# State space tables started after the first u columns; x rows, x^T buffers, row factors and the sine rearranged

## The chip, the cores and the metric

The kernel runs on one NeuronCore of a Trainium2 chip. The metric is the device time of one launch in microseconds. One core has five engines with a queue of instructions each: TensorE (PE; its weight loads are listed as PEld), VectorE (DVE), ScalarE (ACT), GpSimd (POOL) and SyncE (SP), which here issues nearly all DMAs. Each engine takes its own instructions in their order; an instruction that waits holds up everything behind it on that engine.

## The reference, cut to what matters

One layer of a decoder trunk on x of 2048 tokens by 1024 columns, all in float32:

```
h    = RMSNorm(x); P = h @ W_in              # columns for three groups of heads
o_A  = sliding window attention (window 128) of P's columns a
o_B  = S5 state space mixer of P's columns u (512 of them, 32 groups of 16 channels, 64 complex states each)
o_C  = compressed + selected + window attention of P's columns b and c
x    = x + concat(norm(o_A), norm(o_B), norm(o_C)) @ W_out
x    = x + relu(RMSNorm(x) @ W_up)^2 @ W_down
```

The mixer needs tables that depend on its parameters alone, not on x: dt = exp(log_dt), the powers of A_bar = exp(A dt) (magnitude by an exponential, angle by sine and cosine of 11 doublings of the angle), B_bar = (A_bar - 1)/A * B, and products of C with those powers.

## The kernel before, in words

The order of the instructions is set by a scheduler that follows the order in which the Python code emits steps, lists of steps that `merge` interleaves evenly, and priorities; `tc.high_priority` lets an instruction go earlier. A tile pool with n buffers makes the n+1st tile wait for the release of the first. A pool opened where a closed one lay waits for the users of that memory. DMAs that SP issues also wait, in SP's order, for what their target buffer or their completion counter needs.

`phase_front` (line 81) computes P in two halves of 8 row groups (128 tokens with stride 16 each). For one row group, `load_h` (line 103) loads the transposed block of x (`xT`, 512 KB, from a copy of x transposed beforehand) and splits it into a rounded part `hh` (ACT, line 109) and a rest `hl` (DVE, line 110). `load_w` does the same for a column chunk of W_in, one of 8 row blocks k at a time: `raw` by DMA, `wh` (ACT, line 146), `wl` (DVE, line 147). `product` (line 151) multiplies a row group with a chunk: 24 matmuls, three for each k, into one of two PSUM buffers, which ACT then empties. The chunks of a half come in the order u (256 columns), u (256), a (384), b (384), c (396).

The normalising factor of each token is applied to the product. Its sum of squares comes from the rows of x themselves (`row_sum`, line 113, a load and an ACT square per row group), the reciprocal root of 8 row groups from `row_factors` (line 118, 14 small instructions on GpSimd). In the first half the u columns are stored unscaled, and `scaled` (line 122) multiplies them afterwards.

`ssm_tables` (line 282) is a generator with 12 stops. Before, its first eight parts are merged with the first chunk's steps of the first half, and the other four with the second chunk's. `exp_acc` (line 229) is the exponential on DVE (once on 32 columns, names e1..., once on 544, names e2...), `sincos` (line 254) reduces the angle on DVE and calls the sine on ACT twice, for sine and for cosine. `pair_steps` (line 431) then makes, for 16 pairs of groups, the product tables oCA (three DVE instructions of 128x544 each, lines 442 to 444), two matmuls pk with the table k_Y (line 451) and their stores; it is merged with the chunks a, b and c. `extra` makes six bias vectors, one matmul each, after the second chunk.

In the second half, `ssm_steps` (line 467) uses the tables. All later phases (attention, output product, the two products of the feed forward) follow.

Of the kernel before, what the change touches and what calls it, by code (L numbers as in the profile page):

```python
# [7 lines left out]
F32 = mybir.dt.float32  # L8
F32R = mybir.dt.float32r
I32 = mybir.dt.int32  # L10
AF = mybir.ActivationFunctionType
ALU = mybir.AluOpType
# [4 lines left out]
P = 128  # L17
D = 1024
# [17 lines left out]
G = 32  # L36
WIDTHS = {"a": 390, "b": 388, "c": 398}
TWO_PI = 2.0 * math.pi
# [18 lines left out]
def rsqrt_into(nc, pool, y, ss, scale, n, tag, eng=None):  # L57
    h = pool.tile([P, n], F32, tag=tag + "h", name=tag + "h")
    t = pool.tile([P, n], F32, tag=tag + "t", name=tag + "t")
    rsqrt_steps(eng or nc.vector, y, ss, h, t, scale)  # L60


def run(steps):
    for st in steps:
        st()


def merge(*lists):

    order = sorted(((k + 0.5) / len(l), n, k) for n, l in enumerate(lists) for k in range(len(l)))  # L70
    return [lists[n][k] for _, n, k in order]
# [9 lines left out]
def phase_front(tc, C, x, norm1_g, w_in, u_st, pd, rh_a, prm, dkp, dca, consts, extra, x_t):  # L81

    nc = tc.nc
    with ExitStack() as ctx:
        kp = ctx.enter_context(tc.tile_pool(name="skp", bufs=1))
# [31 lines left out]

        def row_factors(half):
            sl = slice(8 * half, 8 * half + 8)
            rsqrt_into(nc, rp, rx[:, sl], ss[:, sl], 1.0 / D, 8, "rq", nc.gpsimd)  # L120

        def scaled(s):
            u = u_st[:, :, u_cols(s)]
# [58 lines left out]
        S = {}  # L182
        for half in range(2):
            box, hs = {}, []

            def steps_of(ch):
                kind, c0, n = ch
                res = [lambda: box.update({ch: load_w(half, *ch)})]
                if ch is chunks[0]:
                    res.insert(0, lambda: hs.append(load_h(8 * half)))  # L190
                for j in range(8):
                    if ch is chunks[0] and j < 7:
                        res.append(lambda j=j: hs.append(load_h(8 * half + j + 1)))
                    for part in ((0, 1) if half and kind != "u" else (None,)):
                        res.append(lambda j=j, part=part: product(8 * half + j, hs[j], box[ch], kind, c0, n, part))
                return res
            lists = [steps_of(ch) for ch in chunks]
            with tc.tile_pool(name=f"a_x{half}", bufs=2, **({} if half else {"reuse_waits": "tile"})) as xp:
                box_x[:] = [xp]
                if half:  # L200
                    run(lists[0] + lists[1] + lists[2][:1])
                else:
                    gen = ssm_tables(tc, C, S, kp, prm, dkp)
                    run(lists[0][:3] + [consts] + merge(lists[0][3:], [lambda: next(gen)] * TABLE_PARTS[0]))
                if half:
                    nc.vector.tensor_copy(xp.tile([1, 1], F32, name="gate", bufs=1), box[chunks[2]][3][1][0:1, 0:1].bitcast(F32))
            if half == 0:
                c_rp = ctx.enter_context(ExitStack())
                rp = c_rp.enter_context(tc.tile_pool(name="a_r", bufs=2, reuse_waits="tile"))
                sums = [[lambda s=s: row_sum(s) for s in range(8 * n, 8 * n + 8)] + [lambda n=n: row_factors(n)] for n in range(2)]  # L210
                scales = [lambda s=s: scaled(s) for s in range(8)]
                run(merge(lists[1], sums[0], [lambda: next(gen, None)] * TABLE_PARTS[1]))
                with tc.tile_pool(name="bv", bufs=1, reuse_waits="tile") as bv:
                    extra(bv, ps_t)
                c_pre = ctx.enter_context(ExitStack())
                pre = c_pre.enter_context(tc.tile_pool(name="pre", bufs=1, side="right", reuse_waits="tile"))
                pairs = pair_steps(tc, C, S, dkp, dca, pre, ps_g)
                run(merge(merge(lists[2], scales) + merge(lists[3], sums[1]) + lists[4], pairs))
                c_rp.close()
            else:  # L220
                c_pre.close()
                tp = ctx.enter_context(tc.tile_pool(name="sg", bufs=2))
                lists[3].insert(8, lambda: head_norms(nc, rh_a, *hn_tiles(sp, "hn"), (pd["a"], 384, 6)))
                rest = sum(lists[2:], [])[1:]
                run(merge(rest, ssm_steps(tc, C, S, u_st, dkp, dca, tp, ps_g, ps_t)))
                store(0)
# [24 lines left out]
    return k  # L251


def sincos(nc, pool, s, c, x, shape, tag):

    def tl(n):
        return pool.tile(shape, F32, tag=tag + n, name=tag + n)
    k, r = tl("k"), tl("r")
    magic = 12582912.0
    nc.vector.tensor_scalar(k, x, 1.0 / TWO_PI, magic, op0=ALU.mult, op1=ALU.add)  # L260
    nc.vector.tensor_scalar(k, k, magic, None, op0=ALU.subtract)
    c1 = 6.28125
    c2 = float(int((TWO_PI - c1) * 2.0 ** 20)) / 2.0 ** 20
    c3 = TWO_PI - c1 - c2
    nc.vector.scalar_tensor_tensor(r, k, -c1, x, op0=ALU.mult, op1=ALU.add)
    nc.vector.scalar_tensor_tensor(r, k, -c2, r, op0=ALU.mult, op1=ALU.add)
    nc.vector.scalar_tensor_tensor(r, k, -c3, r, op0=ALU.mult, op1=ALU.add)
    pi = 3.1415925
    nc.vector.tensor_scalar(r, r, pi, -pi, op0=ALU.min, op1=ALU.max)
    nc.scalar.activation(s, r, AF.Sin)  # L270
    nc.vector.tensor_scalar(r, r, math.pi / 2.0, None, op0=ALU.add)
    nc.vector.tensor_scalar(k, r, pi, -TWO_PI, op0=ALU.is_gt, op1=ALU.mult)
    nc.vector.tensor_tensor(r, r, k, op=ALU.add)
    nc.vector.tensor_scalar(r, r, pi, -pi, op0=ALU.min, op1=ALU.max)
    nc.scalar.activation(c, r, AF.Sin)


TABLE_PARTS = (8, 4)
# [3 lines left out]
def ssm_tables(tc, C, S, pool, prm, dkp):  # L282
# [17 lines left out]
    def tmp(shape, n):  # L300
        return tp.tile(shape, F32, tag="t_" + n, name="t_" + n)

    with ExitStack() as ctx:
        tp = ctx.enter_context(tc.tile_pool(name="si", bufs=1))
        sn, cs = tmp([P, 11, G], "sn"), tmp([P, 11, G], "cs")

        ar, ai, ldt = tmp([P, G], "ar"), tmp([P, G], "ai"), tmp([P, G], "ldt")
        nc.sync.dma_start(ldt, log_dt[0:1].to_broadcast([P, G]))
# [17 lines left out]
        th = tmp([P, 11, G], "th")  # L326
        for j in range(11):
            nc.vector.tensor_scalar(th[:, j], adi, float(2 ** j), None, op0=ALU.mult)
        sincos(nc, tp, sn, cs, th, [P, 11, G], "sc")

        yield
        pr, pi_ = (tp.tile([P, 17, G], F32, tag="e2" + n, name="t_p" + n) for n in ("xc", "r"))
# [98 lines left out]
def pair_steps(tc, C, S, dkp, dca, tp, ps):  # L431
# [5 lines left out]
    def outer(b):  # L437
        bc = [P, GB, 17, 16]
        CA = M["c", b] = tp.tile(bc, F32, tag="oCA", name=f"oCA{b}", bufs=4)
        t1 = tp.tile(bc, F32, tag="ot", name=f"ot{b}", bufs=2)  # L440
        ar, ai = (S[n][:, :, group_slice(b)].rearrange("p t g -> p g t").unsqueeze(3).broadcast_to(bc) for n in ("AR", "AI"))
        nc.vector.tensor_tensor(CA, ar, S["C1"][:, group_slice(b)].unsqueeze(2).broadcast_to(bc), op=ALU.mult)
        nc.vector.tensor_tensor(t1, ai, S["C2"][:, group_slice(b)].unsqueeze(2).broadcast_to(bc), op=ALU.mult)
        nc.vector.tensor_tensor(CA, CA, t1, op=ALU.add)
# [1421 lines left out]
```

## Time and profile before

| | |
|---|---|
| median of 3 runs | 2589.37 us (2584.4 to 2590.45) |
| profiled execution, its own time | 2586.87 us |
| its span, first to last instruction | 2585.0 us |
| busy: PE, PEld | 2468.3 us (95%), 2073.2 us (80%) |
| busy: DVE, ACT, POOL | 1787.2 us (69%), 1334.9 us (52%), 1044.5 us (40%) |
| mean granted TensorE clock | 0.982 |

The span is divided into 40 slices of 64.6 us in the page. TensorE is at 9 tenths or more in nearly all of them; the first slice, 6 tenths, and the second, 8, are the start of `phase_front`. DVE is at 8 and 6 tenths there.

How to read it: busy shares are averages over stages. A wait is put down to what came last by the profile. Matmuls are pipelined and their ends are modelled, so the start of the next one tells more than the duration. An engine's idle time matters only where another waits for what stands behind it.

### The profile page before, as it was taken

The page shows a single profiled execution, that of the slowest core. Times are in us where ns is not written, and L with a number is a line of the kernel's source. Part 1 is how long each engine was busy: PE and PEld are TensorE (multiplying, and loading weights), DVE is VectorE, ACT ScalarE, POOL GpSimd, SP SyncE. Part 2 cuts the span into 40 slices and gives each one's busy share as a digit, 9 for nine tenths or more (in the row PEclk, how much of TensorE's full clock was granted, in tenths as well). Part 3 has the DMA queues.
Part 4 walks back from the last instruction along what each step waited for, and adds up shares of the span by engine and source line. Part 5 has one row for each costly group of instructions (what it writes and reads, how often), then busy time and mean ns, then how long its engine had stood idle before and what let it go on. Part 6 is the DMA issues. An engine that isn't in the chain of part 4 may idle for free. (4 is left out here: it accounts for less than half of the span.)

```text
span 2585.0 us, 38037 instructions
## 1 busy us (share of the span) xinstructions
PE 2468.3 (95%) x12766; PEld 2073.2 (80%) x12766; DVE 1787.2 (69%) x3466; ACT 1334.9 (52%) x2767; POOL 1044.5 (40%) x1047
## 2 busy tenths in 40 slices
PE   6899999999899999999989999899999999999999
PEld 6799997777787777778868888688887888888887
DVE  8643876864776677787566565755557887898886
ACT  4453555754666656565455554544444443344442
POOL 0100222221333333233366667565655354454447
PEclk8999999999899999999999999999999999999999
DMA  6463435321312112121356667755447534444335
GB/s 186 139 205 94 111 95 155 97 69 46 119 40 70 66 46 86 51 66 56 121 191 195 199 184 207 221 166 153 145 131 248 167 102 131 135 131 127 122 102 196
DMA packets 391075, 334.06 MB, mean 129 GB/s; under 512 B 42166, under 2 KB 355132, under 8 KB 389056
## 3 DMA queue, kind: packets, MB, share of 16 engines
q1 hardware_dynamic: 353696, 305.42, 38.9%
q10 hardware_dynamic: 37184, 26.22, 3.1%
q8 instruction: 101, 1.65, 0.3%
q14 instruction: 94, 0.77, 0.1%
HBM read 219.10 MB, written 112.45 MB: 128 GB/s over the span
## 5 line engine op out<-in xcount | busy, mean ns | idle before, releaser
L1341 ACT CAST v<-vr 128x512 fp32r<-128x512 f32 x224 | 139.3, 624 | 303.1 <-DMA vr<-vd 139.6
L1342 DVE TENSOR_TENSOR v<-vr,v 128x512 fp32r<-128x512 f32 x224 | 233.3, 1049 | 78.9 <-ACT v L1341 76.5
L1656 PE MATMUL pdc<-dw,v 128*128 128x512 f32 x768 | 186.3, 392 | 5.4 <-ACT dw L1341 4.1
L1656 PE MATMUL pda<-dw,v 128*128 128x512 f32 x768 | 184.5, 389 | 0.0
L1656 PE MATMUL pdb<-dw,v 128*128 128x512 f32 x768 | 184.5, 389 | 0.0
L1656 PEld LDWEIGHTS pdc<-dw,v 128*128 128x128 f32 x768 | 144.9, 189 | 36.8 <-ACT dw L1341 4.5
L1656 PEld LDWEIGHTS pdb<-dw,v 128*128 128x128 f32 x768 | 144.1, 188 | 30.0
L1656 PEld LDWEIGHTS pda<-dw,v 128*128 128x128 f32 x768 | 144.1, 188 | 30.0
L1452 POOL TENSOR_TENSOR fs<-ur,ur 128x512 f32<-128x512 f32 x64 | 96.8, 1512 | 163.9 <-DMA ur<-in_w_up 117.4
L1341 ACT CAST uh<-fs 128x512 fp32r<-128x512 f32 x128 | 78.6, 621 | 150.1 <-PE pub L1481 64.0
L1342 DVE TENSOR_TENSOR ul<-fs,uh 128x512 fp32r<-128x512 f32 x128 | 134.9, 1057 | 19.6 <-ACT uh L1341 19.5
L1342 DVE TENSOR_TENSOR ul<-ur,uh 128x512 fp32r<-128x512 f32 x96 | 98.8, 1032 | 50.3 <-ACT uh L1341 43.6
L76 PE MATMUL pw<-wo_h,mh 128*128 128x512 f32 x256 | 110.4, 431 | 4.7 <-DVE ml L1211 2.5
L546 POOL TENSOR_TENSOR t<-Q,E 128x508 f32<-128x508 f32 x16 | 21.4, 1341 | 230.9 <-ACT Q L526 200.2
L864 DVE TENSOR_TENSOR tls<-pps,ths 128x512 fp32r<-128x512 f32 (+1 forms) x144 | 92.8, 658 | 29.9 <-ACT ths L863 22.2
L1497 POOL TENSOR_TENSOR ev<-e,e 128x512 f32<-128x512 f32 x64 | 94.9, 1483 | 38.3 <-ACT e L1494 28.1
L863 ACT CAST ths<-pps 128x512 fp32r<-128x512 f32 (+1 forms) x144 | 79.2, 565 | 57.4 <-PE pps L860 26.6
L1481 PE MATMUL pub<-fl,uh 128*128 128x512 f32 x256 | 102.5, 401 | 3.3 <-DVE fl L1342 3.3
L77 PE MATMUL pw<-wo_l,mh 128*128 128x512 f32 x256 | 105.0, 410 | 0.0
L78 PE MATMUL pw<-wo_h,ml 128*128 128x512 f32 x256 | 104.7, 410 | 0.0
L1481 PE MATMUL pub<-fh,uh 128*128 128x512 f32 x256 | 102.8, 401 | 1.2 <-ACT fh L1341 1.2
L1481 PE MATMUL pua<-fh,uh 128*128 128x512 f32 x256 | 101.3, 396 | 2.3 <-ACT e L1501 2.3
(562 smaller groups left out, 7886.2 us busy)
## 6 DMA issues: line engine op xcount, KB each, us to landing
vr<-vd SPq DMA_DIRECT2D x224, 256.0 KB
ur<-in_w_up SPq DMA_DIRECT2D x128, 256.0 KB
vd<-ev SPq DMA_DIRECT2D x128, 256.0 KB
vd<-e ACTq DMA_DIRECT2D x64, 256.0 KB
dr<-in_w_down SPq DMA_DIRECT2D x32, 512.0 KB
x<-in_x SPq DMA_DIRECT2D x16, 512.0 KB
mx<-in_x SPq DMA_DIRECT2D x16, 512.0 KB
x<-mx ACTq DMA_DIRECT2D x16, 512.0 KB
```

Of the source, the lines that this page charges most:

```text
L76: nc.tensor.matmul(out, sh, mh, start=first, stop=False)
L77: nc.tensor.matmul(out, sh, ml, start=False, stop=False)
L78: nc.tensor.matmul(out, sl, mh, start=False, stop=last)
L546: nc.gpsimd.tensor_tensor(t[:, :, :, 0:n], Q[:, :, :, 0:n], e.rearrange("p g j c -> p j g c")[:, :, :, 0:n], op=ALU.mult)
L863: nc.scalar.copy(th[:, 0:nb], pt[:, 0:nb])
L864: nc.vector.tensor_tensor(tl[:, 0:nb], pt[:, 0:nb], th[:, 0:nb], op=ALU.subtract)
L1341: nc.scalar.copy(dh, src)
L1342: nc.vector.tensor_tensor(dl, src, dh, op=ALU.subtract)
L1452: nc.gpsimd.tensor_tensor(t, x, y, op=op)
L1481: nc.tensor.matmul(bank[b], w[:, k], h[o][:, k], start=first and k == 0 and n == 0, stop=k == HALF - 1 and n == 2, skip_group_check=True)
L1497: nc.gpsimd.tensor_tensor(tile_("v" + o), x, y, op=op)
L1656: nc.tensor.matmul(bank[b, q], x[:, q, j], y[:, j], start=first and j == 0 and n == 0, stop=j == 1 and n == 2, skip_group_check=True)
```

## The change

The tables now begin behind the whole first chunk, merged with the second chunk (eight parts) and with the first half of the chunk a (four parts); the pairs are merged with what is left of a, and with b and c. The pool of the x rows moves to the other side of SBUF, so it no longer lies where the x^T pool was, and its loads are merged from the second chunk on as before. The x^T pool has three buffers in the first half. The row factors are made by VectorE, with high priority. Sine and cosine are one ACT instruction on 704 columns. The buffer `ot` of the pairs is single, and their pool closes before the second half begins.

```diff
         def row_factors(half):
             sl = slice(8 * half, 8 * half + 8)
-            rsqrt_into(nc, rp, rx[:, sl], ss[:, sl], 1.0 / D, 8, "rq", nc.gpsimd)
+            with tc.high_priority(offset=W_HOIST):
+                rsqrt_into(nc, rp, rx[:, sl], ss[:, sl], 1.0 / D, 8, "rq")
...
-            with tc.tile_pool(name=f"a_x{half}", bufs=2, **({} if half else {"reuse_waits": "tile"})) as xp:
+            with tc.tile_pool(name=f"a_x{half}", bufs=2 if half else 3, **({} if half else {"reuse_waits": "tile"})) as xp:
                 box_x[:] = [xp]
                 if half:
                     run(lists[0] + lists[1] + lists[2][:1])
                 else:
-                    gen = ssm_tables(tc, C, S, kp, prm, dkp)
-                    run(lists[0][:3] + [consts] + merge(lists[0][3:], [lambda: next(gen)] * TABLE_PARTS[0]))
+                    run(lists[0])
...
             if half == 0:
-                c_rp = ctx.enter_context(ExitStack())
-                rp = c_rp.enter_context(tc.tile_pool(name="a_r", bufs=2, reuse_waits="tile"))
+                c_rp, c_pre = (ctx.enter_context(ExitStack()) for _ in range(2))
+                rp = c_rp.enter_context(tc.tile_pool(name="a_r", bufs=2, side="right", reuse_waits="tile"))
                 sums = [[lambda s=s: row_sum(s) for s in range(8 * n, 8 * n + 8)] + [lambda n=n: row_factors(n)] for n in range(2)]
                 scales = [lambda s=s: scaled(s) for s in range(8)]
-                run(merge(lists[1], sums[0], [lambda: next(gen, None)] * TABLE_PARTS[1]))
+                gen = ssm_tables(tc, C, S, kp, prm, dkp)
+                consts()
+                run(merge(lists[1], sums[0], [lambda: next(gen)] * TABLE_PARTS[0]))
+                l2 = merge(lists[2], scales)
+                n2 = len(l2) // 2
+                run(merge(l2[:n2], [lambda: next(gen, None)] * TABLE_PARTS[1]))
                 with tc.tile_pool(name="bv", bufs=1, reuse_waits="tile") as bv:
                     extra(bv, ps_t)
-                c_pre = ctx.enter_context(ExitStack())
                 pre = c_pre.enter_context(tc.tile_pool(name="pre", bufs=1, side="right", reuse_waits="tile"))
                 pairs = pair_steps(tc, C, S, dkp, dca, pre, ps_g)
-                run(merge(merge(lists[2], scales) + merge(lists[3], sums[1]) + lists[4], pairs))
+                run(merge(l2[n2:] + merge(lists[3], sums[1]) + lists[4], pairs))
+                c_pre.close()
                 c_rp.close()
             else:
-                c_pre.close()
...
-def sincos(nc, pool, s, c, x, shape, tag):
+def sincos(nc, pool, out, x, shape, tag):
...
-    nc.scalar.activation(s, r, AF.Sin)
-    nc.vector.tensor_scalar(r, r, math.pi / 2.0, None, op0=ALU.add)
-    nc.vector.tensor_scalar(k, r, pi, -TWO_PI, op0=ALU.is_gt, op1=ALU.mult)
-    nc.vector.tensor_tensor(r, r, k, op=ALU.add)
-    nc.vector.tensor_scalar(r, r, pi, -pi, op0=ALU.min, op1=ALU.max)
-    nc.scalar.activation(c, r, AF.Sin)
+    nc.vector.tensor_scalar(rc, r, math.pi / 2.0, None, op0=ALU.add)
+    nc.vector.tensor_scalar(k, rc, pi, -TWO_PI, op0=ALU.is_gt, op1=ALU.mult)
+    nc.vector.tensor_tensor(rc, rc, k, op=ALU.add)
+    nc.vector.tensor_scalar(rc, rc, pi, -pi, op0=ALU.min, op1=ALU.max)
+    nc.scalar.activation(out, rr, AF.Sin)
...
-        t1 = tp.tile(bc, F32, tag="ot", name=f"ot{b}", bufs=2)
+        t1 = tp.tile(bc, F32, tag="ot", name=f"ot{b}", bufs=1)
```

What that does to the order shows at three places. From the start of the second half on, every engine has the same instructions in the same order as before.

VectorE, the last two row groups of the first chunk. The names hl are the rests of x^T (numbers count tiles), e2 and sc belong to the second exponential and to the sine. Before:

```order
L274 TENSOR_SCALAR scr<-scr 128x352
L244 TENSOR_TENSOR e2t<-e2p,e2r 128x544
L110 TENSOR_TENSOR hl_455<-xT_453,hh_454 128x1024
L245 TENSOR_SCALAR e2p<-e2t 128x544
L335 MEMSET t_pr 128x32
L347 COPY t_pr<-t_sn 128x32
L246 TENSOR_SCALAR e2t<-e2k 128x544
L341 TENSOR_TENSOR t_t_462<-t_pr,t_sn 128x32
L352 TENSOR_SCALAR t_sn<-t_sn 64x224
L247 CAST e2xc<-e2t 128x544
L110 TENSOR_TENSOR hl_568<-xT_566,hh_567 128x1024
```

VectorE now, the same place, down to the first instructions of the first exponential:

```order
L110 TENSOR_TENSOR hl_298<-xT_296,hh_297 128x1024
L110 TENSOR_TENSOR hl_330<-xT_328,hh_329 128x1024
L148 SCALAR_TENSOR_TENSOR wl_u_2_449<-wr_u_2_446,g_112,wh_u_2_448 128x256
L148 SCALAR_TENSOR_TENSOR wl_u_3_455<-wr_u_3_452,g_112,wh_u_3_454 128x256
L110 TENSOR_TENSOR hl_362<-xT_360,hh_361 128x1024
L240 TENSOR_SCALAR e1xc<-t_ldt 128x32
L241 TENSOR_SCALAR e1k<-e1xc 128x32
```

The whole of the tables has moved behind the last hl (hl_362 is the eighth row group's).

ScalarE near the end of the second u chunk. The names pm_u are the u products in PSUM, rx the row factors, x the rows being squared. Before:

```order
L146 ACTIVATE wh_a_3_1047<-wr_a_3_1045,g_112 128x384
L164 ACTIVATE u_st<-pm_u_810 128x16x16
L124 ACTIVATE u_st<-u_st,rx 128x32x16 x3
L164 ACTIVATE u_st<-pm_u_839 128x16x16
L124 ACTIVATE u_st<-u_st,rx 128x32x16 x2
L116 ACTIVATE x_1480,ss<-x_1480 128x1024
L164 ACTIVATE u_st<-pm_u_870 128x16x16
```

ScalarE now (pm_u_712, 775, 851 are the fifth to seventh products of the second chunk):

```order
L165 ACTIVATE u_st<-pm_u_712 128x16x16
L116 ACTIVATE x_1486,ss<-x_1486 128x1024
L125 ACTIVATE u_st<-u_st,rx 128x32x16
L278 ACT_TABLE_LOAD
L278 ACTIVATE t_sc<-scr 128x704
L165 ACTIVATE u_st<-pm_u_775 128x16x16
L125 ACTIVATE u_st<-u_st,rx 128x32x16 x3
L165 ACTIVATE u_st<-pm_u_851 128x16x16
L147 ACTIVATE wh_a_4_968<-wr_a_4_966,g_112 128x384
```

The first scaling stood behind the fourth product of the second chunk; it now stands behind the fifth, with the sine and its table load behind it.

TensorE, where the first product pk of the pairs stands. Before, it is in the first row group of the chunk a:

```order
L76 MATMUL pm_a_1081<-wh_a_5_1059,hh_120 128x384
L77 MATMUL pm_a_1081<-wl_a_5_1060,hh_120 128x384
L78 MATMUL pm_a_1081<-wh_a_5_1059,hl_121 128x384
L451 MATMUL pk_1117<-oCA_1075,k_Y 128x256 x2
L76 MATMUL pm_a_1123<-wh_a_0_1029,hh_169 128x384
```

TensorE now, where it is in the seventh row group of a, behind 18 of its 24 matmuls:

```order
L77 MATMUL pm_a_1294<-wl_a_5_975,hh_329 128x384
L78 MATMUL pm_a_1294<-wh_a_5_974,hl_330 128x384
L455 MATMUL pk_1242<-oCA_1200,k_Y 128x256 x2
L455 MATMUL pk_1287<-oCA_1237,k_Y 128x256 x2
L76 MATMUL pm_a_1294<-wh_a_6_980,hh_329 128x384
```

All 16 pairs and the six bias vector products now stand from there on.

## Rows read from the trace of the kernel before

**Rows 1.** The page, part 1: busy time, share and instructions of each engine.
```profile
PE 2468.3 (95%) x12766; PEld 2073.2 (80%) x12766; DVE 1787.2 (69%) x3466; ACT 1334.9 (52%) x2767; POOL 1044.5 (40%) x1047
```
**Rows 2.** Busy time by stretch: PE, PEld, DVE, ACT, POOL; clock; DMA share, GB/s.
```profile
7.80:86.30 78.50, 57.23 (x385) 54.39 (x386) 66.81 (x204) 39.90 (x74) 9.05 (x14) 0.85 0.54 160
86.30:208.00 121.70, 121.70 (x654) 113.65 (x653) 62.37 (x119) 61.91 (x117) 3.40 (x14) 1.00 0.60 184
```
**Rows 3.** TensorE's waits, 0 to 208 us: total, times, longest us.
```profile
PE pm_u L78 <- DVE hl L110: 8.4, 4, 6.1
PE pm_u L76 <- ACT u_st L164: 8.1, 1, 8.1
PE pm_u L76 <- ACT wh_u L146: 3.1, 2, 2.9
```
**Rows 4.** TensorE in order of time: start, us, instruction, [idle before and releaser].
```profile
40.41 0.58 PE L78 MATMUL pm_u<-wh_u,hl 128*128 128x256 f32 x1 [6.13 <-DVE hl L110]
...
45.44 0.28 PE L76 MATMUL pm_u<-wh_u,hh 128*128 128x256 f32 x1
...
78.53 0.58 PE L76 MATMUL pm_u<-wh_u,hh 128*128 128x256 f32 x1 [8.07 <-ACT u_st L164]
...
86.26 0.34 PE L76 MATMUL pm_a<-wh_a,hh 128*128 128x384 f32 x1
...
89.24 0.34 PE L78 MATMUL pm_a<-wh_a,hl 128*128 128x384 f32 x1
...
208.05 0.28 PE L76 MATMUL pm_u<-wh_u,hh 128*128 128x256 f32 x1
...
232.89 0.28 PE L78 MATMUL pm_u<-wh_u,hl 128*128 128x256 f32 x1
```
**Rows 5.** SP's queue, ACT and POOL in order of time.
```profile
22.16 0.33 SPq L108 DMA_DIRECT2D xT<-in_x_t  x1
25.65 1.05 ACT L109 CAST hh<-xT 128x1024 fp32r<-128x1024 f32 x1 [1.75 <-DMA xT<-in_x_t]
33.75 1.28 ACT L270 ACT_TABLE_LOAD   x1
38.62 0.50 ACT L275 ACTIVATE t_cs<-scr 128x352 f32<-128x352 f32 x1 [2.69 <-DVE scr L274]
40.42 3.19 SPq L115 DMA_DIRECT2D x<-in_x  x2
70.14 3.26 POOL L51 TENSOR_TENSOR rqt<-rx 128x8 f32<-128x8 f32 x1
76.26 1.94 ACT L124 ACTIVATE u_st<-u_st,rx 128x512 f32<-128x512 f32 x3 [8.97 <-POOL rx L54]
```
**Rows 6.** Busy time by stretch, as rows 2, of four more.
```profile
12.36:86.40 74.04, 53.08 (x372) 51.04 (x372) 62.71 (x196) 35.74 (x66) 9.05 (x14) 0.84 0.54 162
0.00:10.00 10.00, 1.89 (x5) 1.09 (x5) 2.82 (x11) 4.10 (x8) 0.20 (x4) 1.00 0.78 220
60.00:70.00 10.00, 10.00 (x85) 9.91 (x85) 9.56 (x28) 4.66 (x10) 3.15 (x10) 1.00 0.79 254
42.00:44.00 2.00, 2.00 (x12) 2.00 (x11) 2.00 (x4) 0.00 (x0) 0.00 (x0) 0.50 0.56 221
```
**Rows 7.** VectorE's groups, 12.36 to 86.40 us: busy, mean ns, idle before.
```profile
L110 DVE TENSOR_TENSOR hl<-xT,hh 128x1024 fp32r<-128x1024 f32 x7 | 8.5, 1220 | 1.9 <-ACT hh L109 1.9
L147 DVE SCALAR_TENSOR_TENSOR wl_u<-wr_u,g,wh_u 128x256 fp32r<-128x256 f32 x8 | 3.8, 479 | 0.0
L147 DVE SCALAR_TENSOR_TENSOR wl_a<-wr_a,g,wh_a 128x384 fp32r<-128x384 f32 x6 | 3.5, 605 | 7.9 <-ACT wh_a L146 7.9
L443 DVE TENSOR_TENSOR ot<-k_AI,k_C 128x544 f32<-128x544 f32 x3 | 2.1, 707 | 0.0
L340 DVE TENSOR_TENSOR t_t<-t_pxc,t_cs 128x32 f32<-128x32 f32 x1 | 0.2, 184 | 0.0
```
**Rows 8.** VectorE's sums for the a rows, 86 to 140 us, as rows 7.
```profile
L171 DVE TENSOR_REDUCE po_a<-sq_a 128x6 f32<-128x384 f32 x8 | 4.4, 548 | 8.0 <-ACT sq_a L170 8.0
```

More of the change, by code (lines that the diff above doesn't have):

```diff
@@ L251, in exp_acc @@
     return k
-def sincos(nc, pool, s, c, x, shape, tag):
-    def tl(n):
-        return pool.tile(shape, F32, tag=tag + n, name=tag + n)
-    k, r = tl("k"), tl("r")
+def sincos(nc, pool, out, x, shape, tag):
+    k = pool.tile(shape, F32, tag=tag + "k", name=tag + "k")
+    rr = pool.tile([shape[0], 2] + shape[1:], F32, tag=tag + "r", name=tag + "r")
+    r, rc = rr[:, 0], rr[:, 1]
     magic = 12582912.0
@@ L304, in ssm_tables @@
         tp = ctx.enter_context(tc.tile_pool(name="si", bufs=1))
-        sn, cs = tmp([P, 11, G], "sn"), tmp([P, 11, G], "cs")
+        sc = tmp([P, 2, 11, G], "sc")
+        sn, cs = sc[:, 0], sc[:, 1]
         ar, ai, ldt = tmp([P, G], "ar"), tmp([P, G], "ai"), tmp([P, G], "ldt")
@@ L328, in ssm_tables @@
             nc.vector.tensor_scalar(th[:, j], adi, float(2 ** j), None, op0=ALU.mult)
-        sincos(nc, tp, sn, cs, th, [P, 11, G], "sc")
+        sincos(nc, tp, sc, th, [P, 11, G], "sc")
         yield
```

## The prediction

> **What bounds the kernel now.** I read the busy shares first, then TensorE's busy time by stretch, then its waits in the first 208 us, then the order of time on the engine that each wait names. TensorE is the bound: 95% busy [rows 1]. The stretches show where it isn't. From its first matmul to the last u product of the first half (7.8 to 86.3 us) it has 57.2 us of work in 78.5 us; from there to 208 us it is full, 121.7 of 121.7 [rows 2]. So time won before 86.3 us is kept only if the stretch behind stays full in its new order; behind 208 us the order is the same as now, and all of it moves forward.
>
> The floor of the first stretch: 384 matmuls (two chunks, 8 row groups, 24 each). In the second half 210 of the same kind run without a gap from 208.05 to 232.89 us [rows 4], 0.119 us from start to start, so 45.6 us. The other 32.9 us are three long waits, for hl (8.4 us in all, 6.1 the longest), for the emptying of a u product by ScalarE (8.1) and for second-chunk weights (3.1) [rows 3], what each costs in clock afterwards, and the start. For the clock: after the 6.13 us wait TensorE runs 23 matmuls from 40.41 to 45.44 us [rows 4], 0.219 us each, with a granted clock of 0.50 (1.2 GHz) [rows 6]; at 0.119 us they would take 2.7 us, so the slow level costs 2.3 us.
>
> **The change part by part.**
>
> *Tables behind the first chunk.* VectorE's queue now has every hl of the first chunk ahead of the first exponential, so the 6.13 us wait goes. What is late next is the tables, worked out below.
>
> *Third x^T buffer, rows of x in their own place.* Before, a load of x^T waits for the release of one of two buffers, and takes 3.49 us from issue to cast (22.16 to 25.65 us [rows 5]). The first load of x rows is issued at 40.42 us [rows 5], when the x^T pool's place is free. Now both come earlier and share the queue. Ahead of the load of log_dt stand 1.05 MB of first weights, 4.19 MB of x^T, 0.79 MB of second weights (six of eight) and 1.57 MB of x rows: 7.60 MB. At 220 GB/s (the first 10 us) that is 34.5 us, at 254 GB/s (60 to 70 us) 29.9 us [rows 6]. I take 33 us for the first exponential, with 31 and 37 as ends. The Trainium skill (SBUF — State Buffer, section The DMA setup-cost knee) gives a transfer about 2 us and its bytes at 436 GB/s; for 512 KB that is an estimated 3.2 us, near the 3.49 us of the trace, but for the whole queue 17.4 us, which would not hold log_dt back at all. By it the first exponential would start some 2 us earlier and the time be 2572; no 10 us of these rows come near that rate, so the sum goes without it.
>
> *Row factors on VectorE.* GpSimd's chain goes; one of its instructions took 3.26 us [rows 5], and ScalarE sat 8.97 us until it ended [rows 5], which is TensorE's 8.07 us wait [rows 4]. In their place stand 14 instructions on 128x8 for each eight rows. No such row exists on VectorE; the nearest is 0.184 us on 128x32 [rows 7]. Ends: nothing (hidden between others) and 0.55 us (the 128x6 sum [rows 8]); no gain below nothing, since VectorE did none of it. I take 0.184 us, 26 of the 28 ahead of the first pk: 4.8 us. They are queued between table instructions, so ScalarE still waits for them.
>
> *One sine.* Removes one ScalarE instruction of 0.50 us [rows 5]; the one left covers 704 columns instead of 352, so 0.9 us by the same rate (ends 0.5 and 1.0). The table load, 1.28 us [rows 5], stays, but now behind the first row scaling and ahead of the emptying of the sixth product of the second chunk. TensorE's eighth product needs that bank.
>
> *Single ot, earlier close of the pairs' pool.* ot is written and read by VectorE alone, in order: nothing. The pool's place is not used before the second half, whose waits are the same: nothing; if that cover failed, one store's landing, some 3 us.
>
> **The new chain.** VectorE between the first exponential and k_Y, which the first pk needs. Before, that is 12.36 to 86.40 us with 62.7 us busy [rows 6]. Out of it go 8.5 (hl), 3.8 and 3.5 (wl) and the eight pair instructions at 0.707, 5.7 [rows 7]: 41.2 us of tables are left. In the new order stand between the same two: 4 wl of u at 0.479 (1.9), 12 wl of a and b at 0.605 (7.3) and 6 pair instructions (4.2) [rows 7], 6 sums at 0.548 (3.3) [rows 8], and the row factors, 4.8. Together 62.7 us again. Added up along the order by the same durations, wl 6 of the second chunk ends 7.5 us into this, the last row factor at 23.7, the last wl of a at 34.
>
> VectorE's own waits in it: for the sine. Row factors end at 33 + 23.7 = 56.7; a scaling (1.94/3 = 0.65 [rows 5]), the table load and the sine follow, to 59.5, and VectorE, with 1.8 us of other work, is there at 58.5. With the semaphores and the weights of a that wait behind the scalings on ScalarE I put 2 us (ends 0 and 6). k_Y is done at 33 + 62.7 + 2 = 97.7 us.
>
> TensorE's side. The first chunk ends at about 36 (the start as now, eight products at 2.85, 1.5 for emptyings behind squares of x rows). The first product of the second chunk waits for wl 6 and 7, at 33 + 7.5 and one half microsecond each, to 42. The next six products need 17, with a slow stretch 18, so 60; the eighth waits about 1 us for its bank behind the sine, to 64. The first a product then waits for the last wl of a, at 33 + 34 + 1, and ends at 69. An a product is 24 matmuls at 0.175 us (86.26 to 89.24 us holds 17 steps [rows 4]), 4.2 us. Five more and 18 matmuls of the seventh: 93.2 us. So TensorE is there first, waits 4.5 us for VectorE, and passes at 97.7.
>
> In the kernel before, the same 162 a matmuls behind 86.26 us end at 86.26 + 28.4 = 114.7, not counting pk and bias products, all of which the new order has behind this place. The gain there is 114.7 - 97.7 = 17.0 us. Off it go 2 us for the slow clock behind a 4.5 us wait (2.3 behind 6.13 us), and 1 us for the chunk b, whose last two weights stand in SP's queue behind bias-vector stores that wait for TensorE. What is left is 14 us. From the profiled execution's 2586.87 us that is 2572.9; the median of the runs is 2589.37, which would give 2575.4. I take **2574**.
>
> **The rivals.**
>
> *VectorE keeps up.* log_dt lands at 31 or before, and the in-order waits hide. Then TensorE passes at 94, gain 20.7, no slow clock: 2566. For: 254 GB/s [rows 6] with margin at the start. Against: 62.7 us of work have no slack in them, and three waits are in the chain.
>
> *The chain starts late.* 37 us, with 6 us of waits: k_Y at 105.7, gain 9, less 3: 2581. For: x rows stand ahead of log_dt in SP's queue, and the loads of b stand behind the fourth a store. Against: by the same sums the fourth a sum stands at 86, the loads of b land by 91, and their first use stands at 94.
>
> *Slower.* One mechanism: VectorE's in-order queue at the first exponential and at the row factors. If the loads come no earlier than now, the last hl but one ends at 40.4, where TensorE's wait ends [rows 4], the last by estimate a product's length later, 43.2, log_dt follows a load time later, 46.7, and k_Y is at 46.7 + 62.7 + 2 = 111.4; with the 3 us behind it the gain is nought. That is the point from which it turns: k_Y behind 111.7 us. The eight x rows of the second half, 4.2 MB, 16.5 us at 254 GB/s, share SP's queue with the loads of b; with half of that on the chain too it is 8 us slower, 2595. Against: the third buffer alone takes away the wait that set the 43.2.
>
> *It does not do what it says.* The loads are the limit already, and a third buffer moves nothing: the same 46.7, no change, 2588.
>
> **How the numbers follow.** The forecast case (gain 10 to 18) has 0.55, VectorE keeps up 0.17, the late start 0.20, slower 0.05, nothing moved 0.03. A difference under 0.3%, 7.8 us, cannot be told from no change. Faster by more than that: the first two and half of the third, 0.82. Within it: the other half and nothing moved, 0.13. Slower: 0.05. The range takes in both neighbours with their bounds, 37 and 31 us for the start, 0 and 6 us of waits, 0 to 0.55 us for a row factor instruction: 2565 to 2583. The forecast case's own is 2569 to 2578.
>
> **What would show it.** In the new profile there should be no wait over 2 us for hl in the first chunk; the first exponential at 31 to 37 us, just behind the last hl; the first product of the chunk a at 63 to 67 us instead of 86.26; no GpSimd instruction before the second half; a wait of TensorE (or a long pk) at the first pk, 95 to 101 us, with VectorE's k_Y just ahead; the second half's first u product at 191 to 198 us instead of 208.05; and the same length from there to the end. If the first pk has no wait, the chain was shorter than I added up. I am wrong if the second half starts less than 8 us earlier, or if what it gains is not found at the end of the span.

## The result, and the profile after

The changed kernel took 2573.7 us (median; 2571.7 to 2576.3), where the kernel before took 2589.9: a ratio of 0.9942, 95% interval 0.9925 to 0.996. Timed again on another chip (the run e9 below) it took 2574.6 against 2586.8, ratio 0.9957 (0.9943 to 0.9972). It is faster by 12 to 16 us. The forecast was 2574. One execution of e4 below, of 6100 us at a granted clock of 0.43, is in no figure here.

First the busy shares and the stretches of the changed kernel, which answer to [rows 1] and [rows 2] (busy time of PE, PEld, DVE, ACT, POOL with counts; granted clock; DMA share; GB/s).

```profile
PE 2468.9 (96%) x12766; PEld 2072.4 (81%) x12766; DVE 1795.6 (70%) x3494; ACT 1332.4 (52%) x2766; POOL 1036.5 (40%) x1019
```

```profile
7.88:61.65 53.77, 50.81 (x385) 49.10 (x386) 41.78 (x130) 37.52 (x70) 0.00 (x0) 1.00 0.75 239
61.65:95.29 33.64, 28.99 (x164) 28.04 (x163) 32.38 (x112) 18.72 (x36) 0.00 (x0) 0.99 0.59 159
95.29:105.00 9.71, 9.71 (x36) 8.89 (x37) 7.00 (x14) 3.11 (x6) 0.00 (x0) 0.69 0.30 103
105.00:192.72 87.72, 87.14 (x456) 78.95 (x455) 50.49 (x97) 41.88 (x79) 0.00 (x0) 1.00 0.58 180
```

The same 384 u matmuls that took 78.5 us now take 53.8, at a granted clock of 1.00, with the DMA engines at 239 GB/s instead of 160. What is new stands in the third line: 9.7 us at a clock of 0.69.

TensorE's waits of the changed kernel up to 208 us (total, times, longest), for [rows 3]; the first line is the start of the program:

```profile
PE pm_u L76 <- ACT hh L109: 7.9, 1, 7.9
PE pk L455 <- DVE k_Y L412: 3.5, 1, 3.5
PE pm_u L76 <- ACT u_st L165: 1.9, 1, 1.9
```

The long waits of before (8.4 us in four, 8.1 in one, 3.1 in two) have become one of 1.9 and a new one of 3.5, for k_Y. The milestones, in order of time over the engines (start, us, instruction, idle before and releaser), for [rows 4, 5]:

```profile
31.28 0.18 DVE L240 TENSOR_SCALAR e1xc<-t_ldt 128x32 f32<-128x32 f32 x1 [3.21 <-DMA t_ldt<-in_ssm_log_dt]
...
55.53 0.73 ACT L125 ACTIVATE u_st<-u_st,rx 128x512 f32<-128x512 f32 x1 [1.11 <-DVE rx L54]
...
57.57 0.79 ACT L278 ACTIVATE t_sc<-scr 128x704 f32<-128x704 f32 x1
...
61.65 0.34 PE L76 MATMUL pm_a<-wh_a,hh 128*128 128x384 f32 x1
...
94.56 0.67 DVE L412 TENSOR_TENSOR k_Y<-t_v,t_v 128x512 f32<-128x512 f32 x1
...
95.29 3.78 PE L455 MATMUL pk<-oCA,k_Y 128*128 128x256 f32 x8 [3.50 <-DVE k_Y L412]
...
192.72 0.28 PE L76 MATMUL pm_u<-wh_u,hh 128*128 128x256 f32 x1
```

The second half starts at 192.72 instead of 208.05 us, 15.3 earlier; the span is 13.2 shorter. The missing 2.1 us are lost far behind the change, in the feed forward. Its first matmul comes 15.6 us earlier than before, the last of its first product 13.1 (kernel before, then changed kernel):

```profile
1320.74 0.39 PE L1481 MATMUL pua<-fh,uh 128*128 128x512 f32 x1
...
1963.23 0.40 PE L1481 MATMUL pub<-fh,ul 128*128 128x512 f32 x1
```

```profile
1305.15 0.39 PE L1485 MATMUL pua<-fh,uh 128*128 128x512 f32 x1
...
1950.18 0.40 PE L1485 MATMUL pub<-fh,ul 128*128 128x512 f32 x1
```

Part of it is probably the clock: in the same 40 us behind the start of the second half (from 1648 us before and 1633 us now) it was 0.87 before and is 0.83 now, some 1.6 us by estimate. What loses the rest is not shown.

### The profile page after: what moved, and what is told of

Its sections match the earlier page's. It is cut to its first block, busy times and chain, and to the rows that moved or that the text cites. A ratio compares the mean times of both kernels' runs of the same rounds, so it can differ in the third digit from the quotient of the medians.

```text
span 2571.8 us, 38051 instructions
## 1 busy us (share of the span) xinstructions
PE 2468.9 (96%) x12766; PEld 2072.4 (81%) x12766; DVE 1795.6 (70%) x3494; ACT 1332.4 (52%) x2766; POOL 1036.5 (40%) x1019
## 3 DMA queue, kind: packets, MB, share of 16 engines
q8 instruction: 101, 1.65, 0.3%
## 5 line engine op out<-in xcount | busy, mean ns | idle before, releaser
L868 DVE TENSOR_TENSOR tls<-pps,ths 128x512 fp32r<-128x512 f32 (+1 forms) x144 | 92.8, 657 | 30.3 <-ACT ths L867 22.6
L867 ACT CAST ths<-pps 128x512 fp32r<-128x512 f32 (+1 forms) x144 | 79.0, 565 | 58.6 <-PE pps L864 27.5
```

Source lines behind the costliest of these rows:

```text
L867: nc.scalar.copy(th[:, 0:nb], pt[:, 0:nb])
L868: nc.vector.tensor_tensor(tl[:, 0:nb], pt[:, 0:nb], th[:, 0:nb], op=ALU.subtract)
```

## The experiments

All but e12 are the changed kernel with an edit or two. Each was timed beside the kernel before on its own chip (e1 to e4, e5 to e8 and e9 to e12 on three chips, where that took 2585.7, 2585.6 and 2586.8 us). The columns: ratio to the kernel before, then from one trace the first exponential, the first pk, TensorE's wait ahead of it, and the second half's first u product, in us.

| run | ratio (95%) | e1xc | pk | wait | half 2 |
|---|---|---|---|---|---|
| before | 1 | 12.4 | - | - | 208.05 |
| changed | 0.9942 (0.9925-0.996) | 31.3 | 95.3 | 3.50 | 192.72 |
| e9 changed again | 0.9957 (0.9943-0.9972) | 30.9 | 94.0 | 3.45 | 190.15 |
| e1 parameters early | 0.9964 (0.9952-0.9976) | 27.5 | 92.8 | 3.32 | 192.77 |
| e2 second factors on GpSimd | 0.9948 (0.9935-0.996) | 31.1 | 94.0 | 3.09 | 190.14 |
| e3 all factors on GpSimd | 0.9971 (0.996-0.9982) | 30.2 | 101.2 | 2.95 | 197.49 |
| e4 two x^T buffers | 0.9983 (0.9971-0.9995) | 39.7 | 104.1 | 3.46 | 200.74 |
| e5 turns behind pairs | 0.9978 (0.9964-0.9992) | 30.5 | 97.6 | none | 193.91 |
| e6 rows of x left | 0.9948 (0.9927-0.9969) | 31.6 | 95.3 | 1.60 | 190.40 |
| e7 tables in front | 1.0008 (0.9994-1.0022) | 12.4 | 92.1 | none | 207.53 |
| e8 two sines | 0.9936 (0.9915-0.9958) | 30.8 | 93.4 | 3.13 | 188.06 |
| e10 two sines, second factors | 0.9939 (0.9924-0.9954) | 30.6 | 93.4 | 3.23 | 189.63 |
| e11 as e10, loads of b early | 0.9935 (0.992-0.9951) | 31.0 | 93.4 | 3.09 | 188.18 |
| e12 tables only | 0.9987 (0.9977-0.9997) | 38.6 | 107.0 | 3.21 | 200.26 |

**e9, the same kernel again.** No edit.

> The changed kernel itself, on the chip of the other runs. Theory (its gain is in the front of the program; the rest, the same instructions, varies by some us from execution to execution): first pk, wait and second half as in its first profile, 95.3, 3.5 and 192.7 us, within 1 us but for the 1.2 GHz stretch behind the wait, which may be shorter (two runs with waits of 2.95 and 3.13 us had one and had none), so second half at 189.5 to 193; ratio to before 0.9935 to 0.996. Rival (the gain measured first belonged to that chip): ratio over 0.997.

The theory holds, and the run sets the measure for all others: the second half of the same program started 2.6 us earlier in this trace (k_Y 1.3 earlier, the slow stretch behind the wait shorter). Differences of that size between two traces show nothing. Of the rest of the program, the same work in all these kernels, the traces (e5 left out) show 2372 to 2384 us, the one of before 2377. And the runs of e1 to e12 gain 1 to 9 us less, mostly 2 to 6, than the second half's start gains on 208.05; since that is common to all, it probably lies in the one trace of before, which was not taken again.

**e1, parameters early.**

```
+ ar, ai, ldt = keep([P, G], "ar"), keep([P, G], "ai"), keep([P, G], "ldt")   # loads behind them, then yield
+ run(lists[0]); next(gen)                                                    # ahead of the second chunk's steps
```

> The changed kernel, but log_dt, a_re and a_im have a place of their own and are loaded behind the fourth x^T instead of behind two rows of x. Theory (VectorE's chain from the landing of log_dt to k_Y sets the first pk): the first exponential starts when VectorE is through the last hl and two wl, at about 28.5 us instead of 31.3; k_Y ends at about 92.5 instead of 95.2; TensorE's wait of 3.5 us at the first pk shrinks to about 1 and the 1.2 GHz stretch behind it goes or shrinks; the second half's first u product at 188 to 190 us instead of 192.7; the run at 2569 to 2571 where the changed kernel has 2573.7. Rival (the end of the chain hangs on something else, as the loads of b, or TensorE is late itself by then): first exponential earlier, k_Y and the second half where they were, 2573 to 2574.

The rival, for a reason neither named. The chain started 3.8 us earlier and k_Y was 2.5 earlier than in the first trace. But in SP's queue the second chunk's weights went back (the first from 12.10 to 20.76 us, the fifth and sixth from 25.47 to 31.38, now behind a load for C too), and TensorE waited there; its first a product began at 62.86 instead of 61.65:

```profile
PE pk L457 <- DVE k_Y L414: 3.3, 1, 3.3
PE pm_u L76 <- ACT wh_u L147: 2.6, 2, 2.2
```

The first pk also stands earlier among the a products here, so that its time and the wait ahead of it do not compare one to one.

**e2, second row factors on GpSimd.**

```
- rsqrt_into(nc, rp, rx[:, sl], ss[:, sl], 1.0 / D, 8, "rq")
+ rsqrt_into(nc, rp, rx[:, sl], ss[:, sl], 1.0 / D, 8, "rq", nc.gpsimd if half else nc.vector)
```

> The changed kernel, but the second eight rows' factors, which are needed only in the second half, are on GpSimd. This takes 14 instructions of 0.16 us (2.3 us) out of VectorE's queue ahead of k_Y and changes nothing else of the chain. Theory (VectorE's queue sets the first pk): k_Y ends at 92.9 instead of 95.2, TensorE's wait at the first pk 1.2 instead of 3.5 us, second half at 189 to 190.5, run at 2570 to 2571.5. Rival (the loads of b, which are issued when the tables' place is free, or TensorE set it): wait and second half unchanged, 2573 to 2574.

At first sight the second half (190.14) bears the theory out. Beside e9 (190.15) it falls: without the 14 instructions, the first pk comes at 94.00 us, with them at 93.97. VectorE's rows of the first and last instructions of Ea show why; in e9, with row factors (L44 to L54) between them:

```profile
81.47 0.24 DVE L365 TENSOR_TENSOR t_t<-k_Ea,t_sc 128x32 f32<-128x32 f32 x1
81.60 0.23 DVE L366 TENSOR_TENSOR t_t<-k_Ea,t_sc 128x32 f32<-128x32 f32 x1
81.72 0.20 DVE L44 TENSOR_SCALAR rqh<-ss 128x8 f32<-128x8 f32 x1
81.87 0.22 DVE L367 TENSOR_TENSOR k_Ea<-t_t,t_t 128x32 f32<-128x32 f32 x1
...
86.33 0.40 DVE L370 TENSOR_TENSOR k_Ea<-t_t,t_t 128x128 f32<-128x128 f32 x1
```

In e2, without them:

```profile
81.57 0.22 DVE L365 TENSOR_TENSOR t_t<-k_Ea,t_sc 128x32 f32<-128x32 f32 x1
81.70 0.22 DVE L366 TENSOR_TENSOR t_t<-k_Ea,t_sc 128x32 f32<-128x32 f32 x1
81.95 0.23 DVE L367 TENSOR_TENSOR k_Ea<-t_t,t_t 128x32 f32<-128x32 f32 x1
...
86.35 0.41 DVE L370 TENSOR_TENSOR k_Ea<-t_t,t_t 128x128 f32<-128x128 f32 x1
```

L366 does not need L365 and starts 0.13 us behind it, while L365 still runs; L367 needs L366 and starts 0.25 behind it. The row factors sit in that gap: from the first of these rows to the end of the last it is 5.26 us with twelve of them and 5.19 without. They cost nothing. The Trainium skill (VectorE: DVE Perf Modes, section The DRAIN you can't avoid) says that an operation waits until the pipe in front of it is empty, and that one which is not held starts earlier; these rows agree with the second half of that, and show what the gap is good for.

That is so for the second eight rows. The first eight rows' factors stand among instructions that do not wait for the one in front, and there each puts the next one back. Two places in e9, with such a factor (L51) behind a table instruction and without:

```profile
47.95 0.52 DVE L271 SCALAR_TENSOR_TENSOR scr<-sck,scr 128x352 f32<-128x352 f32 x1
48.39 0.16 DVE L51 TENSOR_TENSOR rqt<-rx 128x8 f32<-128x8 f32 x1
48.47 0.72 DVE L248 TENSOR_TENSOR e2t<-e2p,e2r 128x544 f32<-128x544 f32 x1
```

```profile
45.45 0.52 DVE L269 SCALAR_TENSOR_TENSOR scr<-sck,t_th 128x352 f32<-128x352 f32 x1
45.89 0.72 DVE L248 TENSOR_TENSOR e2t<-e2p,e2r 128x544 f32<-128x544 f32 x1
```

L248 starts 0.52 us behind the instruction ahead of the factor, and 0.44 us where there is none; 14 times 0.08 is some 1.1 us, an estimate. No run takes these alone out of VectorE's queue without making the row scaling later.

**e3, all row factors on GpSimd.** The diff's `rsqrt_into(..., nc.gpsimd)` without the priority, as before.

> The changed kernel with one part undone: both row factors on GpSimd as before. GpSimd's chain took 10.1 us before, VectorE's 6.8 now, so the first row scaling would come 3.4 us later (58.9), the sine and the emptying of the u product behind it as well, TensorE's wait there 5.3 instead of 1.9 us, with 1.2 GHz behind it. VectorE is rid of 4.5 us of work but waits for the sine longer. Theory (two chains that are near each other at the first pk: what TensorE loses earlier is mostly taken from its wait at the first pk): TensorE at the first pk about 95 to 97, k_Y about 96, second half 193.5 to 195.5, run at 2575 to 2577. Rival (the wait for GpSimd's factors, 8.07 us before, comes back whole): second half at about 199, run at 2580 to 2582.

In between: at 197.49 the second half is 4.8 to 7.3 us later than the changed kernel's two traces, and the rival's mechanism is the one in the trace. GpSimd's third instruction and the row scaling behind the chain:

```profile
50.02 4.92 POOL L51 TENSOR_TENSOR rqt<-rx 128x8 f32<-128x8 f32 x1
```

```profile
58.56 0.72 ACT L124 ACTIVATE u_st<-u_st,rx 128x512 f32<-128x512 f32 x1 [9.38 <-POOL rx L54]
```

ScalarE stood 9.4 us, though the scaling began only 3 to 4 us later than with VectorE's factors: what stood in ScalarE's queue behind it (the emptying of u products) had to wait from the last square on, and TensorE with it for 8.6 us. The theory, which counted the delay of the scaling alone, missed that.

**e4, two x^T buffers.** `bufs=2` instead of `2 if half else 3` for the pool of x^T.

> The changed kernel with one part undone: two x^T buffers. Then x^T loads wait for a buffer's release again, and in SP's queue three or four rows of x (0.52 MB each) and two tables stand ahead of log_dt that stood behind it. Theory (what stands ahead of log_dt in the queue sets the chain's start): about 1.8 MB more ahead of it, 7 us at 250 GB/s; first exponential at 37 to 39 us, k_Y at 101 to 103, TensorE waits 6 us or more at the first pk or comes later itself; second half at 199 to 201, run at 2580 to 2582. Rival (the loads limit the first chunk anyway, the third buffer moves nothing): first exponential within 1 us of 31.3, run at 2573 to 2575.

The theory: 39.7 us for the first exponential (a little over its 37 to 39), second half at 200.74. The waits for hl that one buffer less brings are small (2.0 us in three); the third buffer is worth 8 to 11 us (against 192.72 and 190.15). With two, SP waited 10.5 us for hl ahead of x^T loads instead of 5.4, and the last hl came at 35.53 instead of 26.85. The load of log_dt was issued at 36.78, when that hl ended, and not when so many bytes had passed, as the theory has it (see the second step below).

**e5, turns behind the pairs.** The block that fills Eb and Ea moves from ahead of qr, qi to the chunk c; b_re and b_im load into places of the exponential:

```
- run(merge(l2[n2:] + merge(lists[3], sums[1]) + lists[4], pairs))
+ run(merge(l2[n2:] + merge(lists[3], sums[1]) + merge(lists[4], [lambda: next(gen, None)] * 2), pairs))
- B1, B2 = tmp([P, G, 16], "B1"), tmp([P, G, 16], "B2")
+ B1, B2 = (tp.tile([P, G, 16], F32, tag="e2" + n, name="t_B" + n) for n in ("p", "t"))
```

> The changed kernel with the tables in another order: k_Y is worked out right behind AR and AI, and the two tables of turns (Ea and Eb, 14.4 us of VectorE instructions in the changed kernel, needed only in the second half) behind it, among the chunk c. The loads of b stand in places of exponentials that are free by then. Theory (the first pk waits only for VectorE's in-order queue): k_Y ends at 78 to 84 us instead of 95.2, TensorE has no wait over 1 us at the first pk and no 1.2 GHz stretch behind it; that gives back 3.5 us of wait and about 3 us of clock (9.71 us from 95.29 on had a granted clock of 0.69); second half at 185 to 188 us instead of 192.7; ratio to the kernel before about 0.9917 where the changed kernel has 0.9942. Rival (another wait is right behind: ScalarE's emptying, weights of b in SP's queue): second half at 189 to 193, ratio as the changed kernel's.

The theory's mechanism is there: k_Y ends at 72 us, and TensorE has no wait and no slow clock at the first pk. The time is the rival's and worse, by other waits than either named. SP's queue:

```profile
44.25 0.42 SPq L404 DMA_DIRECT2D dkp<-t_zz  x1
56.49 0.47 SPq L379 DMA_DIRECT2D t_Bp<-in_ssm_b_re  x1
...
58.98 1.00 SPq L140 DMA_DIRECT2D wr_a<-in_w_in  x2
...
188.28 0.33 SPq L108 DMA_DIRECT2D xT<-in_x_t  x1
```

SP stood still for 12 us, until the place of b was free, and chunk a's weights stood behind it: 7.3 us of TensorE's waits, with a granted clock of 0.83 from 60 to 80 us and 0.90 from there to the first pk (its waits from 50 to 100 us):

```profile
PE pm_a L77 <- DVE wl_a L148: 3.7, 2, 2.9
PE pm_a L76 <- ACT wh_a L147: 3.6, 2, 2.5
```

And the second half's first x^T, which the changed kernel issues at 144.97, is issued at 188.28, so that its first two chunks take 51.7 us (193.91 to 245.65) instead of 46.6.

**e6, rows of x left.** `side="right"` taken out of the pool of the rows.

> The changed kernel with one part undone: the rows of x have no place of their own, but that of the x^T pool, and so load only behind the last hl (26.85 us). Then log_dt stands behind less in the queue, the rows later. Theory (the eighth row of x sets the row factors, these the sine and the u emptying): first exponential at 28 to 30 us instead of 31.3, eighth square at 50 to 52 instead of 47.5, first row scaling at 57.5 to 59.5 instead of 55.5, TensorE's wait for the emptying at 4 to 6 us instead of 1.9, second half at 194 to 197 instead of 192.7, run 2 to 4 us longer. Rival (k_Y alone sets the end of the front): with the earlier first exponential k_Y at 93 to 94, second half at 190 to 192, run no longer.

Neither: the row scaling came 6.7 us later (62.24 instead of 55.53), as the theory has it and more, but the second half started at 190.40, no later than in e9, and the ratio is the changed kernel's. ScalarE's order had changed with it: the sine and the emptying now stand ahead of the scaling, and TensorE's waits for the emptying were two of 0.8 us. No gain from the rows' own place shows; but since ScalarE's order changed with it, the run does not undo the place alone.

**e7, tables in front.** The tables' first eight parts merged with the first chunk again, two x^T buffers; the rest of the change stays.

> The changed kernel with the tables begun within the first chunk again, as before; since their place then takes that of the third x^T buffer, there are two. Row factors by VectorE and the one sine stay. Theory (tables ahead of the hl are what costs most): TensorE waits for hl again, 6 to 8 us in all with 2 us of clock, no wait at the first pk; the rows of x stand behind the tables' loads in the queue and the emptying waits too; second half at 201 to 206 us where the changed kernel has 192.7 and the kernel before 208.05; ratio to before 0.9965 to 0.999. Rival (row factors on GpSimd were the main loss): the 8.07 us wait for the emptying is gone and most of the gain with it is there, second half at 194 to 198.

Slower than both: no gain at all (1.0008, 0.9994 to 1.0022). TensorE's waits from 8 to 208 us:

```profile
PE pm_u L77 <- DVE wl_u L148: 10.5, 1, 10.5
...
PE pm_u L78 <- DVE hl L110: 8.0, 3, 6.2
```

The wait for the emptying is gone, as the rival said, and one of 10.5 us for second-chunk weights, behind the tables in VectorE's queue, has its place. With the tables in front, the parts that are left (the third buffer is not among them) gain nothing.

**e8, two sines.**

```
+ nc.scalar.activation(out[:, 0], r, AF.Sin)      # ahead of the cosine's reduction
- nc.scalar.activation(out, rr, AF.Sin)
+ nc.scalar.activation(out[:, 1], rc, AF.Sin)
```

> The changed kernel with two sine instructions of 352 columns, the first in ScalarE's queue ahead of the last square of the second rows. One more instruction (0.50 us where the two took 1.0 before, one of 704 columns takes 0.79 now). Theory (the sine itself is short, and stands behind the row scaling anyway): VectorE gets the sines 0 to 1 us later, second half within 1 us of 192.7, run 2573 to 2575. Rival (ScalarE, in order, stands still until VectorE has the first sine's argument, and the emptying behind it with it): TensorE's wait for the emptying grows by 2 us or more and the second half starts 2 to 4 us later.

Neither: the second half starts at 188.06, 4.7 us earlier than in the first trace of the changed kernel and 2.1 earlier than in e9. ScalarE's rows:

```profile
52.57 1.28 ACT L274 ACT_TABLE_LOAD   x1
53.87 0.50 ACT L274 ACTIVATE t_sc<-scr 128x352 f32<-128x352 f32 x1
...
55.58 0.71 ACT L125 ACTIVATE u_st<-u_st,rx 128x512 f32<-128x512 f32 x1
56.19 0.48 ACT L279 ACTIVATE t_sc<-scr 128x352 f32<-128x352 f32 x1
```

The table load and the first sine now lie ahead of the row scaling, and the second is done at 56.67, where the one sine was done at 58.36 and, in e9, at 57.11. k_Y is 1.9 us earlier than in the first trace and 0.6 than in e9; the other 2.7 and 1.5 us are the clock, which did not fall: the same 3 us of changed kernel, e8, and e3 behind its own pk, PE alone:

```profile
96.00:99.00 3.00, 3.00 (x9) 0.50 0.12 48
```

```profile
96.00:99.00 3.00, 3.00 (x18) 1.00 0.51 180
```

```profile
102.00:105.00 3.00, 3.00 (x11) 0.56 0.09 24
```

The 2.1 us are less than the two traces of the changed kernel differ by, and the intervals of the ratios overlap: that two sines are better is likely (in e8, e10 and e11 the second half starts earlier than in e9, e2 and the first trace), but not shown.

**e10 and e11, two combinations.** e10 joins e8 and e2; e11 adds `B1, B2 = keep(...)`, so that b loads early.

> Two sines as in the run of that name and the second row factors on GpSimd. Theory (TensorE's wait at the first pk is VectorE's queue, and 2.3 us of second factors stand in it): k_Y at 90.5 to 91.5 us instead of 93.35 with two sines alone, TensorE's wait at the first pk 0.5 to 1.5 us instead of 3.13, no 1.2 GHz stretch, second half at 185.5 to 187 instead of 188.06, ratio to before 0.9925 to 0.9935. Rival (weights of b or ScalarE are right behind): second half at 187.5 to 188.5, ratio 0.9936 as with two sines alone.

> As the run before, and b_re and b_im in a place of their own, so that they load early and k_Y is worked out right behind Ea, ahead of the first oCA, whose end then is what the first pk waits for. Theory: the end of both 0.5 to 1 us earlier than with the late loads, 90 to 90.5 us; wait at the first pk under 1 us; second half at 185 to 186.5; ratio 0.992 to 0.9935. Rival (d's load, issued behind stores of chunk a, holds VectorE's queue between k_Y and the first oCA): wait of 2 us or more at the first pk, second half at 187.5 or later.

e10's theory falls as e2's did: pk at 93.41, e8 93.35. In e11 k_Y was done at 88.5, 5 us earlier, and the rival's place is the right one though not its cause: five other instructions (two for W, dD, W itself and a row sum) stood between the halves of the first oCA:

```profile
87.84 0.68 DVE L413 TENSOR_TENSOR k_Y<-t_v,t_v 128x512 f32<-128x512 f32 x1
88.43 0.72 DVE L447 TENSOR_TENSOR oCA<-k_AR,k_C 128x544 f32<-128x544 f32 x1
...
92.59 0.70 DVE L449 TENSOR_TENSOR oCA<-oCA,ot 128x544 f32<-128x544 f32 x1
```

e11 beats the kernel before (0.9935) and on the same chip took 2568.3 us, where the changed kernel took 2574.6; four of its five runs lie below all of e9's, but the intervals of the two ratios overlap.

**e12, tables only.** The kernel before with the tables' move alone.

> The kernel before with one part of the change alone: the tables begun behind the first chunk, with two x^T buffers, rows of x behind them, row factors on GpSimd, two sines. Theory (the parts add up: undone one by one they moved the second half's start by +8.0 for the third buffer, +4.8 for the factors, -2.3 for the rows' place, -4.7 for the one sine): second half at 197 to 200 us where the changed kernel has 192.7 and the kernel before 208.05, with TensorE waiting about 8 us for the emptying; ratio to before 0.996 to 0.998. Rival (the parts need each other; without the third buffer and VectorE's factors the moved tables only move the wait to the first pk): second half at 204 us or later, ratio 0.999 or more.

Nearly the theory: 200.26 us, half of the gain at the second half, with waits at the a weights (3.3 us), k_Y (3.2) and the emptying (2.7, not 8). The ratio, 0.9987, is just outside what it gave: 3.5 us, where the changed kernel gained 12.2 on the same chip.

## Why the prediction was right, step by step

- *Tables behind the first chunk*: right, and shown by e7 and e12. With the tables in front the rest gains nothing; the move alone gives half of the gain at the second half (7.8 of 15.3 us) and less of the time (3.5 of 12.2 us).
- *Third buffer, rows in their own place*: the time was right, 31 us as the early end and 30.9 and 31.3 measured, but by luck: the sum lets 7.60 MB pass ahead of log_dt, and these are not what held it (at most they did so through the x^T loads that the hl wait for). SP waited 1.7 us for the last hl and issued the load when it had ended (26.85 + 1.23 = 28.08 us); 3.2 us later the first exponential began:

```profile
26.85 1.23 DVE L110 TENSOR_TENSOR hl<-xT,hh 128x1024 fp32r<-128x1024 f32 x1 [1.00 <-ACT hh L109]
...
28.10 0.33 SPq L312 DMA_DIRECT2D t_ldt<-in_ssm_log_dt  x1
```

  The tables' pool opens when the x^T pool closes, and this wait shows that it lies in its place. In e9 (27.19 and 27.21), e2, e3, e4, e8, e10 and e11 the load follows the last hl as closely; in e1, where log_dt has a place of its own, it was issued at 5.50 and the first exponential stood right behind the last hl and two wl, at 27.49. The order that holds, last hl and then a load time, is the one that the rival *Slower* is worked out with. The rate that fits, 7.60 MB in 29.6 us (1.65 to 31.28) or 257 GB/s, is near the one at the early end by chance. The Trainium skill (SBUF — State Buffer, section The DMA setup-cost knee) gives a transfer about 2 us and its bytes at 436 GB/s. By it the prediction estimated that the queue would not hold log_dt back. Here it did not, and in two stretches of 2 us (6 to 10 us) the trace has 383 and 413 GB/s. The two edits were taken as one; e4 gives the gain to the buffer, e6 shows none for the place.
- *Row factors on VectorE*: the wait that they replace was right (e3). Their price was the step that failed: 26 times 0.184, 4.8 us of the chain. Those of the second eight rows cost nothing, since they fit between dependent instructions (e2, e10); those of the first eight cost some 1.1 us by the spacing in e9. The lower end of the range, nothing, was nearly right.
- *One sine*: sized right (0.79 us for 0.9). I compared one duration with two and left out that the first of two sines can be ready sooner. In e8 the second half starts 2.1 and 4.7 us earlier than in the changed kernel's two traces, which differ by 2.6 themselves, so whether one sine is better or two stays open.
- *The chain*: 62.7 us of work and 2 of waits; measured from 31.28 to k_Y's end at 95.23: 59.7 us busy and 4.2 idle. The sum is right within 1 us because errors offset each other: 3.0 us too much work (the row factors some 3.7 too much, the rest 0.7 too little) and 2.2 too little for waits and gaps.
- *TensorE's side*: 93.2 us at the first pk (91.8), 4.5 of wait (3.5), 2 of slow clock (2.7: from the first pk to the first b product 10.8 us pass, in e8, with no slow stretch, 8.1). The sign set for the first product of the chunk a, 63 to 67 us, was missed: it came at 61.65, in part because the wait for wl 6 and 7 of the second chunk, some 3 us in the sum, was 0.6.
- *The gain*: 14 us forecast, 15.3 at the second half, 13.2 in the span, 16.2 between the medians (12.2 on the chip of e9). That the median meets 2574 within 0.3 us is luck. The sign that the rest takes the same time was missed by 2.1 us.

## What to carry to other kernels

Ask of an instruction that is added to an in-order queue whether it stands among dependent ones: there a short one was free here, among independent ones it cost 0.08 us. Ask of a DMA that is moved forward whether its target is free at that time: if not, all that SP has behind it stands too, and the bytes ahead of it say little about when it lands. And run the changed kernel twice before a difference of one trace, here 2.6 us, is given to a cause.

## What was not expected of the hardware

Behind waits of TensorE at the first pk of 3.50, 3.46, 3.45, 3.32, 3.23, 3.21, 3.09 (twice) and 2.95 us there was a stretch at 1.2 GHz, behind one of 3.13 (e8) and one of 1.60 (e6) none: the length of the wait alone did not tell. The changed kernel's own two traces, with waits of 3.50 and 3.45 us, differ in it too: from the first pk to the first b product it is 10.8 us in the one and 9.6 in the other. The Trainium skill (TensorE: Matmul & The Clock Gate, Part 1) says that the moment of the change does not hang on the kernel's start and so varies between runs; these rows vary as it says, but do not show why. On GpSimd the same 128x8 multiplication took 4.92 us the first time and 0.20 later in one chain (e3); the profile's spans on GpSimd are rough.
